# A head's softmax moved into the next head's block, a seventh pair in the seven-product phase, and 13 fillers a head in an attention trunk

## The chip, the cores and the metric

The kernel runs on one NeuronCore of a Trainium2 chip. The metric is the device time of one execution in microseconds (us); 2113.32 us is the median of three runs before the change. In this kernel a change under about 0.2% (4.2 us) can't be told from none.

## What is computed

Two layers work on a residual stream x of 1024 positions by 1024 features in float32. Layer 0 mixes by a short gated convolution, layer 1 by dilated attention with 16 heads of 64 dimensions; each is followed by a SwiGLU block of width 2816, and a norm ends the trunk. The change lies in the attention layer:

```python
qkv = (h @ w_qkv).reshape(bsz, seq, 3, N_HEADS, HEAD_DIM)
q, k, v = qkv[:, :, 0], qkv[:, :, 1], qkv[:, :, 2]
for window, dilation in BRANCHES:          # (128, 1), (512, 4), (2048, 16)
    o, l = dilated_branch(q, k, v, rel_bias, window, dilation)   # banded softmax(qk + bias) v, and its log-sum
    outs.append(o); lses.append(l)
alpha = jax.nn.softmax(jnp.stack(lses, axis=0), axis=0)
o = jnp.sum(alpha[..., None] * jnp.stack(outs, axis=0), axis=0)
return o.reshape(bsz, seq, D_MODEL).astype(h.dtype) @ w_out
```

## The kernel before

Activations lie transposed, features on the 128 partitions and positions along the free axis. Every float32 product that must be exact is made of three matmuls: each operand is split into a high and a low part (`split`, line 128: ScalarE copies the high part, VectorE subtracts it), and high by high, high by low and low by high are summed in a PSUM bank. Large products go by Strassen's seven-product scheme (class `Strassen`, products at lines 570 to 572) where two weight tiles can be paired; the rest go through `product` (lines 372 to 374). All instructions stand in the order in which the Python code issues them; each engine takes its own in that order. SBUF tiles come from a pool of 41 pages and some half pages, PSUM has 8 banks.

Q and K of the attention are made for pairs of heads (8 pairs). The class `QueryKey` makes the first `QK_PAIRS` pairs in a seven-product phase: 7 products of 4 k-tiles and 3 terms, 84 matmuls of 128x512 a pair, against 96 by `product`. Its results are scaled, split and written to DRAM by `emit` (lines 1139 to 1148), from where each head's block loads them.

After that come 17 blocks, one call of `slot(n, ...)` each, for n = 0 to 16. Block n holds three strands, interleaved by hand:

- `scores` of head n: score matmuls of q against k in eight steps (lines 1573 and 1574; first against `kca`, k regrouped by residue mod 4 for the two wide branches, then against `ka`), each followed by VectorE's additions of the bias out of the bank into `lf`, `lh`, `ld` and `lp` (lines 1584 to 1615), by maxima into `m`, and at the end by GpSimd's `partition_all_reduce` of m into mb (line 1627);
- `values` of head n-1: matmuls of the exponentials with the values (line 1646), whose sums and denominators ScalarE copies out as z and o (lines 1669 and 1670), which frees two banks;
- fillers, steps of the generator `dense`: the value projections v1 to v3 (20 steps a tile group, lines 1516 to 1518), Q and K of pairs 6 and 7 (`projections`, 36 steps a pair, of which 32 hold three matmuls), and the first half of the output product (`out_product`, 64 steps), whose banks VectorE adds to x at line 491.

`softmax(n)` is five pairs of operations: VectorE subtracts mb from `lf`, `lh`, `ld` and the two parts of `lp` (line 1635), and ScalarE takes the exponential (line 1636). Blocks 0 to 13 (`n <= LAG`) are of the lagged form: a first half of eight score steps with a filler each, and a second half in which the values of head n-1 run among the remaining fillers; there `softmax(n)` is issued at one go in the second half's step 3. From block 14 on scores and values share the first half, and `softmax(n)` stands in the second half's step 4.

`finish` scales a finished pair, `attended` writes it to DRAM, and `load_attended` with `halves` reads the first four pairs back and splits them (tiles `oin` to `w_lo`) ahead of the output product.

Of the kernel before, what the change touches and what calls it, by code (L numbers as in the profile page):

```python
# [20 lines left out]
H = 16  # L21
# [20 lines left out]
FFN_PAIRS, FFN_CHUNK = 9, 3  # L42
CONV_PAIRS, CONV_CHUNK, CO = 0, 1, 4
CONV, QK = "conv", "qk"
QK_PAIRS = 6
PAGES = 41
SOFT = 4
FIN0 = 2
AO_WIDE = 5
AO = 4  # L50
LAG = 13
FILL = (("v", 0), ("v", 1), ("v", 2), ("qk", 6), ("v", 3), ("qk", 7))
DEEP_ORDER = (1, 2, 5, 6, 7, 3, 4)


# [44 lines left out]
def trunk(ctx: ExitStack, tc: tile.TileContext, x, gains_in, cwi, ck, cwo, wqkv, wo, relb,  # L100
# [276 lines left out]
    def run(*gens):  # L377
        for _ in zip(*gens):
            pass
        for g in gens:  # L380
            for _ in g:
                pass
# [1096 lines left out]
    def attention(norm, qk):  # L1479
# [150 lines left out]
        def softmax(st):  # L1630
            lf, lh, ld, lp, mb = (st[n] for n in ("lf", "lh", "ld", "lp", "mb"))
            for dst, m in ((lf, mb), (lh, mb[:, HALF:]), (ld, mb),
                           (view(lp, 8, [[32, 16], [1, 24]]), view(mb, 8, [[32, 16], [1, 24]])),
                           (lp[:, HALF:], mb[:, HALF:])):
                nc.vector.tensor_tensor(out=dst, in0=dst, in1=m, op=ALU.subtract)
                nc.scalar.activation(dst, dst, AF.Exp)
                yield
# [72 lines left out]
                nc.vector.tensor_tensor(out=o, in0=o, in1=z, op=ALU.mult)  # L1710
                nc.gpsimd.dma_start(odram[p], o)

        put_off, ending = [], []
        OZ, acts = {}, {}

        def slot(n, dense, ndense, late=0, hook=iter(())):

            def other(k):
                for _ in range(k):
                    next(dense, None)  # L1720
# [25 lines left out]
            used = 0  # L1746
            if lagged:
                for i in range(8):
                    next(sc, None)
                    if n or i % 2:  # L1750
                        other(1)
                        used += 1
                    if a and ending and i == 0:
                        run(ending.pop())
                run(sc)
            else:
                if a == 0 and not late:
                    other(1)
                    used += 1
                for i in range(8):  # L1760
                    next(sc, None)
                    next(pv, None)
                    next(pv, None)
                    if i >= late and i % 2 == 0:
                        other(1)
                        used += 1
                run(sc)
                run(pv)
                if a == 0:
                    extra = finish(p - 1)  # L1770
                if a == 0 and n < H:
                    load_values(p)
            left = max(ndense - used, 0)
            for i in range(8):
                next(pv, None)
                next(pv, None)
                if i == (2 if n > LAG + 1 else 5):
                    attended()
                if not lagged and (i < FIN0 or i > SOFT):
                    next(extra, None)  # L1780
                if i in (1, 2):
                    next(later, None)
                if i < 4:
                    next(hook, None)
                if i == (3 if lagged else SOFT):
                    if n < H:
                        live[n] = new
                        run(softmax(new))
                other(left * (i + 1) // 8 - left * i // 8)
            run(pv)  # L1790
            run(extra)
# [48 lines left out]

        dense = fill()
        for n in range(H):
            if n == LAG - 1:
                done.update(load_attended(range(AO)))
            hook = halves() if n == LAG - 1 else iter(())
            slot(n, dense, 15, 3 if n == H - 2 else 0, hook)
            run(hook)
        acts.update(split_attended(load_attended(range(AO, 7))))
        ensure(ahead_ao)
        slot(H, dense, 15)  # L1850
        run(dense)
        return acts

# [203 lines left out]
```

## Time and profile before

| what | us |
|---|---|
| median of 3 runs (2112.34 to 2113.49) | 2113.32 |
| the profiled execution | 2113.6 |
| its span | 2111.8 |
| phase that makes Q and K, about 980 to 1095 | 115 |
| first score matmul of head 0 | at 1104.3 |
| first score matmul of head 15 | at 1385.0 |
| DMA share in the head blocks (1104 to 1406) | 0.77 |

The profile names engines PE (TensorE), PEld (its weight loads), DVE (VectorE), ACT (ScalarE), POOL (GpSimd) and SP (SyncE). A row of a single instruction gives its start and length in us, the engine, the line, the operation, the tile written and the tiles read, shape, and in brackets the idle time before it with what ended it. Matmuls are pipelined: a 128x512 matmul shows 0.39 us, but the next one starts 0.23 us later, so work is counted by the distance of starts.

### The profile page before, as it was taken

The page shows a single profiled execution, that of the slowest core. Times are in us where ns is not written, and L with a number is a line of the kernel's source. Part 1 is how long each engine was busy: PE and PEld are TensorE (multiplying, and loading weights), DVE is VectorE, ACT ScalarE, POOL GpSimd, SP SyncE. Part 2 cuts the span into 40 slices and gives each one's busy share as a digit, 9 for nine tenths or more (in the row PEclk, how much of TensorE's full clock was granted, in tenths as well). Part 3 has the DMA queues.
Part 4 walks back from the last instruction along what each step waited for, and adds up shares of the span by engine and source line. Part 5 has one row for each costly group of instructions (what it writes and reads, how often), then busy time and mean ns, then how long its engine had stood idle before and what let it go on. Part 6 is the DMA issues. An engine that isn't in the chain of part 4 may idle for free. (4 is left out here: it accounts for less than half of the span.)

```text
span 2111.8 us, 30764 instructions
## 1 busy us (share of the span) xinstructions
PE 2088.2 (99%) x11006; PEld 1796.4 (85%) x11006; DVE 1737.2 (82%) x3255; ACT 1021.1 (48%) x1868; POOL 236.8 (11%) x337
## 2 busy tenths in 40 slices
PE   9999999999999999999999999999999999999998
PEld 7788888888888888887799999988788888888887
DVE  8898769988888888968967687987998888888876
ACT  7433427443434554446545555555544434456435
POOL 1000000110101000010322222211011011001000
PEclk9999999999999999999999999999999999999999
DMA  7322643323333476351767777955223333358432
GB/s 221 95 95 70 229 135 75 105 100 110 115 100 107 155 206 203 121 157 65 244 210 190 170 184 191 250 190 140 70 90 105 105 106 105 115 187 244 158 95 80
DMA packets 141527, 300.77 MB, mean 142 GB/s; under 512 B 48252, under 2 KB 54478, under 8 KB 141376
## 3 DMA queue, kind: packets, MB, share of 16 engines
q1 hardware_dynamic: 107488, 201.94, 32.7%
q0 software_dynamic: 26256, 82.18, 12.3%
q10 hardware_dynamic: 7632, 14.70, 1.8%
q8 instruction: 87, 1.43, 0.3%
q14 instruction: 64, 0.52, 0.1%
HBM read 208.49 MB, written 82.93 MB: 138 GB/s over the span
## 5 line engine op out<-in xcount | busy, mean ns | idle before, releaser
L572 PE MATMUL bank<-b,w 128*128 128x512 f32 x1952 | 761.3, 390 | 5.1 <-DVE w L145 4.9
L570 PE MATMUL bank<-b,w 128*128 128x512 f32 x1952 | 761.7, 390 | 3.6 <-ACT w L144 2.3
L571 PE MATMUL bank<-b,w 128*128 128x512 f32 x1952 | 761.2, 390 | 0.6 <-DVE b L881 0.6
L572 PEld LDWEIGHTS bank<-b,w 128*128 128x128 f32 x1952 | 366.9, 188 | 85.6 <-DVE w L145 9.4
L570 PEld LDWEIGHTS bank<-b,w 128*128 128x128 f32 x1952 | 367.0, 188 | 80.1 <-ACT w L144 3.1
L571 PEld LDWEIGHTS bank<-b,w 128*128 128x128 f32 x1952 | 367.1, 188 | 75.6 <-DVE b L881 1.5
L144 ACT ACTIVATE w<-combo 128x512 fp32r<-128x512 f32 (+2 forms) x488 | 249.2, 540 | 237.8 <-DVE combo L192 220.6
L145 DVE TENSOR_TENSOR w<-combo,w 128x512 fp32r<-128x512 f32 (+2 forms) x488 | 276.5, 580 | 37.9 <-ACT w L144 37.1
L576 ACT ACTIVATE part<-bank 128x512 f32<-128x512 f32 x186 | 110.7, 595 | 377.7 <-PE bank L572 377.4
L145 DVE TENSOR_TENSOR w<-raw,w 128x512 fp32r<-128x512 f32 (+2 forms) x342 | 189.8, 576 | 36.3 <-ACT w L144 36.3
L580 DVE TENSOR_TENSOR part<-part,bank 128x256 f32<-128x256 f32 (+1 forms) x366 | 170.7, 496 | 29.5 <-PE bank L572 16.7
L144 ACT ACTIVATE w<-raw 128x512 fp32r<-128x512 f32 (+2 forms) x342 | 166.8, 530 | 45.4 <-PE bank L572 11.5
L372 PE MATMUL bank<-w_hi,w 128*128 128x512 f32 (+1 forms) x400 | 150.8, 377 | 0.1
L374 PE MATMUL bank<-w_hi,w 128*128 128x512 f32 (+1 forms) x400 | 149.3, 373 | 0.7 <-DVE w L145 0.7
L373 PE MATMUL bank<-w_lo,w 128*128 128x512 f32 (+1 forms) x400 | 149.0, 372 | 0.0
L491 DVE TENSOR_TENSOR x<-x,bank 128x512 f32<-128x512 f32 (+1 forms) x104 | 66.2, 642 | 61.2 <-PE bank L374 60.8
L800 DVE TENSOR_TENSOR x<-x,bank 128x512 f32<-128x512 f32 x136 | 92.6, 681 | 28.8 <-PE bank L572 28.8
L192 DVE TENSOR_TENSOR combo<-raw 128x512 f32<-128x512 f32 (+1 forms) x172 | 111.1, 647 | 0.0
L374 PEld LDWEIGHTS bank<-w_hi,w 128*128 128x128 f32 x400 | 75.3, 188 | 14.8 <-DVE w L145 1.6
L563 DVE TENSOR_TENSOR b<-hin,b 128x512 fp32r<-128x512 f32 x126 | 79.4, 684 | 9.4 <-ACT b L562 9.4
L372 PEld LDWEIGHTS bank<-w_hi,w 128*128 128x128 f32 x400 | 75.5, 189 | 12.6 <-ACT w L144 0.5
L373 PEld LDWEIGHTS bank<-w_lo,w 128*128 128x128 f32 x400 | 75.5, 189 | 12.1
(241 smaller groups left out, 3452.8 us busy)
## 6 DMA issues: line engine op xcount, KB each, us to landing
hin<-part SPq DMA_DIRECT2D x126, 256.0 KB
raw<-in_ffn_w_gate SPq DMA_DIRECT2D x44, 512.0 KB
raw<-in_ffn_w_up SPq DMA_DIRECT2D x44, 512.0 KB
part<-sum POOLq DMA_DIRECT2D x72, 256.0 KB, 2.3
raw<-in_ffn_w_down SPq DMA_DIRECT2D x48, 384.0 KB
raw<-in_attn_w_qkv SPq DMA_DIRECT2D x27, 512.0 KB
raw<-in_conv_w_in SPq DMA_DIRECT2D x24, 512.0 KB
part<-part POOLq DMA_DIRECT2D x36, 256.0 KB, 2.6
```

Of the source, the lines that this page charges most:

```text
L144: nc.scalar.activation(hi, src, AF.Copy)
L145: eng.tensor_tensor(out=lo, in0=src, in1=hi, op=ALU.subtract)
L192: eng.tensor_tensor(out=c, in0=a, in1=b, op=op)
L372: nc.tensor.matmul(b, whi[:, a], ahi[:, s], start=first, stop=False)
L373: nc.tensor.matmul(b, whi[:, a], alo[:, s], start=False, stop=False)
L374: nc.tensor.matmul(b, wlo[:, a], ahi[:, s], start=False, stop=last)
L570: nc.tensor.matmul(b, hi[:, a], bhi, start=start and k == 0, stop=False, skip_group_check=True)
L571: nc.tensor.matmul(b, hi[:, a], blo, start=False, stop=False, skip_group_check=True)
L572: nc.tensor.matmul(b, lo[:, a], bhi, start=False, stop=k == n - 1, skip_group_check=True)
L576: nc.scalar.activation(t, b, AF.Copy)
L580: nc.vector.tensor_tensor(out=t, in0=t, in1=b, op=ALU.add)
L800: nc.vector.tensor_tensor(out=X[n][:, half(h)], in0=X[n][:, half(h)], in1=b, op=ALU.add)
```

## The change

Three constants change. `QK_PAIRS` goes from 6 to 7, and pair 6 leaves the list of fillers. The fillers per block go from 15 to 13 (`DENSE`), and in a lagged block ten of these stand in the first half: one at each score step and a second one at steps 3 and 7 (`EXTRA`). In the lagged blocks `softmax(n)` is no longer run in block n; its generator is kept in `due` and stepped once ahead of each score step of block n+1. Block 13 still runs it at once, since block 14 has another form. `finish` of the pair before is issued at score step 4 instead of 0. The attended tiles are loaded and split in block 11 instead of 12.

```diff
-QK_PAIRS = 6
+QK_PAIRS = 7
...
-FILL = (("v", 0), ("v", 1), ("v", 2), ("qk", 6), ("v", 3), ("qk", 7))
+EXTRA = (3, 7)
+FILL = (("v", 0), ("v", 1), ("v", 2), ("v", 3), ("qk", 7))
+DENSE = 13
...
-        put_off, ending = [], []
+        put_off, ending, due = [], [], [iter(())]
...
             if lagged:
                 for i in range(8):
+                    next(due[0], None)
                     next(sc, None)
-                    if n or i % 2:
-                        other(1)
-                        used += 1
-                    if a and ending and i == 0:
+                    k = 1 + (i in EXTRA) if n else i % 2
+                    other(k)
+                    used += k
+                    if a and ending and i == 4:
                         run(ending.pop())
...
-                if i == (3 if lagged else SOFT):
-                    if n < H:
-                        live[n] = new
-                        run(softmax(new))
+                if i == (3 if lagged else SOFT) and n < H:
+                    live[n] = new
+                    due[0] = softmax(new)
+                    if n >= LAG:
+                        run(due[0])
...
-            if n == LAG - 1:
+            if n == LAG - 2:
                 done.update(load_attended(range(AO)))
-            hook = halves() if n == LAG - 1 else iter(())
-            slot(n, dense, 15, 3 if n == H - 2 else 0, hook)
+            hook = halves() if n == LAG - 2 else iter(())
+            slot(n, dense, DENSE, 3 if n == H - 2 else 0, hook)
...
-        slot(H, dense, 15)
+        slot(H, dense, DENSE)
```

What this does to the order on the engines, at the three places that the prediction speaks of. Lines of the new kernel are two higher than those of the old one there.

ScalarE, around the end of block 3, before:

```order
L1636 ACTIVATE lf<-lf 128x1024
L1636 ACTIVATE lh<-lh 128x512
L1636 ACTIVATE ld<-ld 128x1024
L1636 ACTIVATE lp<-lp 128x16x24
L1636 ACTIVATE lp<-lp 128x512
L1669 ACTIVATE z<-bank 64x512
L1670 ACTIVATE o<-bank 64x512
L1669 ACTIVATE z<-bank 64x512
L1670 ACTIVATE o<-bank 64x512
```

and in the change:

```order
L1671 ACTIVATE z<-bank 64x512
L1672 ACTIVATE o<-bank 64x512
L1671 ACTIVATE z<-bank 64x512
L1672 ACTIVATE o<-bank 64x512
L1638 ACTIVATE lf<-lf 128x1024
L1523 ACTIVATE v<-bank,scales 128x256
L1638 ACTIVATE lh<-lh 128x512
L1638 ACTIVATE ld<-ld 128x1024
L1638 ACTIVATE lp<-lp 128x16x24
L1638 ACTIVATE lp<-lp 128x512
```

The copies of z and o out of the value banks stood behind the five exponentials of the next head and now stand ahead of them; evictions of the value projection (v) fall among the exponentials.

VectorE, head 0's softmax and the first adds of head 1, before:

```order
L1635 TENSOR_TENSOR lf<-lf,mb 128x1024
L1635 TENSOR_TENSOR lh<-lh,mb 128x512
L1635 TENSOR_TENSOR ld<-ld,mb 128x1024
L1635 TENSOR_TENSOR lp<-lp,mb 128x16x24
L1635 TENSOR_TENSOR lp<-lp,mb 128x512
```

and in the change:

```order
L1637 TENSOR_TENSOR lf<-lf,mb 128x1024
L1586 TENSOR_TENSOR lf<-bank,bias 128x4x64 x2
L1637 TENSOR_TENSOR lh<-lh,mb 128x512
L1586 TENSOR_TENSOR lf<-bank,bias 128x4x64 x2
L1637 TENSOR_TENSOR ld<-ld,mb 128x1024
L1595 TENSOR_TENSOR lh<-bank,bias 128x512
L1600 TENSOR_TENSOR m<-lf,lh 128x512
L1637 TENSOR_TENSOR lp<-lp,mb 128x16x24
L1612 TENSOR_TENSOR ld<-bank,bias 128x16x16
L1617 TENSOR_TENSOR lp<-bank,bias 128x16x16
L1637 TENSOR_TENSOR lp<-lp,mb 128x512
```

The five subtractions stood together; now the bias adds of the next head stand between them. The first subtraction, which waits for the all-reduce, stays ahead of the next head's first add.

VectorE, where the four attended tiles are split, before (ahead of head 12's softmax):

```order
L1624 TENSOR_TENSOR m<-m,lp 128x512
L145 TENSOR_TENSOR w_lo<-oin,w_hi 128x1024 x4
L1635 TENSOR_TENSOR lf<-lf,mb 128x1024
L1635 TENSOR_TENSOR lh<-lh,mb 128x512
L1635 TENSOR_TENSOR ld<-ld,mb 128x1024
```

and in the change (ahead of head 11's):

```order
L1626 TENSOR_TENSOR m<-m,lp 128x512
L147 TENSOR_TENSOR w_lo<-oin,w_hi 128x1024 x4
L1712 TENSOR_TENSOR o<-o,z 128x1024
L1143 SCALAR_TENSOR_TENSOR kq<-bank,rstd 128x512
L1637 TENSOR_TENSOR lf<-lf,mb 128x1024
L1586 TENSOR_TENSOR lf<-bank,bias 128x4x64 x2
L1149 TENSOR_TENSOR kq_lo<-kq,kq_hi 128x512
L1637 TENSOR_TENSOR lh<-lh,mb 128x512
```

A pair's scaling (o by z) and a Q part of pair 7 moved from behind the softmax to ahead of it. On GpSimd's queue the eight DRAM writes of pair 6 move from the head blocks to the phase that makes Q and K; on SyncE's queue its two weight loads move there too, and the loads of four attended tiles come one block earlier.

## The prediction

> **What bounds the kernel now.** I read the busy line first, then the table of stretches, then the waits of TensorE and VectorE in the attention stage, and last single rows in order of time, because a busy share says nothing about which wait ends last.
>
> ```profile
> span 2111.8 us, 30764 instructions
> PE 2088.2 (99%) x11006; PEld 1796.4 (85%) x11006; DVE 1737.2 (82%) x3255; ACT 1021.1 (48%) x1868; POOL 236.8 (11%) x337
> ...
> 980.00:1095.00 115.00, 114.12 (x554) 95.53 (x553) 102.67 (x158) 61.46 (x105) 30.40 (x55) 1.00 0.55 182
> ...
> 1153.50:1175.50 22.00, 20.43 (x161) 20.02 (x160) 16.88 (x29) 14.55 (x22) 5.65 (x7) 0.92 0.72 177
> 1175.50:1251.10 75.60, 75.60 (x562) 71.32 (x561) 58.52 (x104) 40.68 (x57) 21.20 (x20) 1.00 0.81 194
> ...
> PE bank L1573 <- ACT o L1670: 1.6, 2, 1.1
> ```
>
> The stretch rows give length, then busy time of PE, PEld, DVE, ACT and POOL, then the granted clock. TensorE is busy without a gap in the phase that makes Q and K (980 to 1095) and in the head blocks (from 1104), except in one block: 1153.5 to 1175.5 lasts 22.0 us, holds 1.57 us of idle TensorE and a clock of 0.92. Its neighbours carry the same kind of work at clock 1.00. So in both stages a matmul less is time less, as long as the other engines keep up.
>
> ```profile
> 1251.12 0.29 PE L1573 MATMUL bank<-qa,kca 128*128 128x256 f32 x1
> 1269.44 0.29 PE L1573 MATMUL bank<-qa,kca 128*128 128x256 f32 x1
> ...
> 1212.77 0.28 PE L1573 MATMUL bank<-qa,kca 128*128 128x256 f32 x1
> 1232.26 0.28 PE L1573 MATMUL bank<-qa,kca 128*128 128x256 f32 x1
> ...
> 1344.17 0.28 PE L1573 MATMUL bank<-qa,kca 128*128 128x256 f32 x1
> 1364.71 0.28 PE L1573 MATMUL bank<-qa,kca 128*128 128x256 f32 x1
> ```
>
> These are the first score matmuls of neighbouring blocks, so each pair is a block's length: 18.3 us with value fillers (block 8), 19.5 us with Q/K fillers (block 6), 20.5 us with out-product fillers (block 13).
>
> VectorE's loop is next. A head's chain is: subtract the maximum, add the biases to the next head's scores, take maxima, wait for GpSimd's all-reduce, subtract again.
>
> ```profile
> 1117.00 1.23 DVE L1635 TENSOR_TENSOR lf<-lf,mb 128x1024 f32<-128x1024 f32 x1 [3.54 <-POOL mb L1627]
> ...
> 1128.05 0.69 DVE L1624 TENSOR_TENSOR m<-m,lp 128x512 f32<-128x512 f32 x1
> 1132.16 1.23 DVE L1635 TENSOR_TENSOR lf<-lf,mb 128x1024 f32<-128x1024 f32 x1 [3.42 <-POOL mb L1627]
> ...
> DVE lf L1635 <- POOL mb L1627: 38.2, 13, 3.5
> DVE w_lo L145 <- ACT w_hi L144: 8.0, 4, 2.3
> DVE kq_lo L1147 <- ACT kq_hi L1144: 5.6, 5, 1.9
> ```
>
> Without other work one turn is 11.74 us of VectorE (1117.00 to 1128.74) and 3.42 us of waiting, 15.2 us. That is 3.1 us under the shortest block, and every split or scaling that VectorE does beside it eats into this margin.
>
> **The change part by part.** *Pair 6 leaves the fillers.* Its 32 steps with matmuls are three 128x512 matmuls each.
>
> ```profile
> 1227.62 0.48 PE L372 MATMUL bank<-b,w_hi 128*128 128x512 f32 x1
> 1227.93 0.39 PE L373 MATMUL bank<-b,w_hi 128*128 128x512 f32 x1
> 1228.16 0.40 PE L374 MATMUL bank<-b,w_lo 128*128 128x512 f32 x1
> 1228.40 0.38 PE L1646 MATMUL bank<-ld,vx 128*128 128x128 f32 x2
> 1228.62 0.39 PE L1646 MATMUL bank<-lp,vx 128*128 128x128 f32 x2
> ...
> 1229.20 0.48 PE L372 MATMUL bank<-b,w_hi 128*128 128x512 f32 x1
> ```
>
> Two steps start 1.58 us apart, and between them lie four double value matmuls 0.22 us apart, 0.88 us. A step costs 0.70 us, and 32 steps are 22.4 us off TensorE's line. The four steps that only evict carry no matmul.
>
> *Pair 6 enters the seven-product phase* with 84 matmuls (7 products, 4 k-tiles, 3 terms).
>
> ```profile
> 1075.81 0.39 PE L570 MATMUL bank<-b,w 128*128 128x512 f32 x1
> ...
> 1076.49 0.39 PE L570 MATMUL bank<-b,w 128*128 128x512 f32 x1
> ```
>
> Three matmuls start in 0.68 us, so 84 take 19.05 us. VectorE has some 15 us of new work in them (4 sums, 7 splits, 3 partial sums, 4 scalings, 4 low parts, at about 0.69 us, the low part's row further down) and was busy 103 of 115 us in that phase with TensorE at 114, so I put the phase's extra wait at 0; bounds are 0 and 0.9 us, the idle time that the phase has now. The weight DMAs only come earlier. Both moves together: 3.35 us less.
>
> *The softmax steps move between the next block's scores.* The number of instructions is the same. What moves on ScalarE is the place of the eviction of the value sums (z and o), which free two banks.
>
> ```profile
> 1158.60 0.28 PE L1518 MATMUL bank<-w_hi,b 128*128 128x256 f32 x1
> ...
> 1159.94 0.38 PE L1573 MATMUL bank<-qa,ka 128*128 128x256 f32 x1 [1.07 <-ACT o L1670]
> ...
> 1161.17 0.48 PE L1573 MATMUL bank<-qa,ka 128*128 128x256 f32 x1 [0.51 <-ACT o L1670]
> 1161.45 0.42 PE L1574 MATMUL bank<-ql,ka 128*128 128x256 f32 x1
> ...
> 1159.92 0.59 ACT L1669 ACTIVATE z<-bank 64x512 f32<-64x512 f32 x1
> ```
>
> Twice in block 3 TensorE waits for the copies L1670, which stand behind five exponentials that wait for VectorE; then its matmuls take 0.42 instead of 0.28 us for some 3.4 us (the 0.92 above). With the evictions ahead of the exponentials (the order shown in the section on the change) these copies, four of 0.59 us, are done some 2.4 us into the block, before any exponential, and this block should shrink to its neighbours: 22.0 - 18.4 = 3.6 us. Bounds: 0, if the banks run out elsewhere, and 3.6.
>
> That half-speed stretch came after 1.6 us of idle. The Trainium skill, "TensorE: Matmul & The Clock Gate", section on the clock gate, has the array drop to half clock only after an idle window of about 3.4 us. This trace disagrees (0.92 in the row above after two waits of 1.07 and 0.51 us); by the page a wait of some 2 us would cost itself alone.
>
> *Thirteen fillers instead of fifteen a block.* The steps are only spread thinner (220 in place of 256), so TensorE's sum is already counted; what shrinks is the cover over VectorE's loop. A block with value fillers loses two steps of 0.72 us (six matmuls 0.12 us apart), four in five of them with matmuls: 18.3 - 1.15 = 17.2 us. With Q/K it is 19.5 - 1.4 = 18.1, with the out product 20.5 - 1.4 = 19.1 us. The plain loop of 15.2 fits under all of them. The rest that VectorE has to do there:
>
> ```profile
> L1710 DVE TENSOR_TENSOR o<-o,z 128x1024 f32<-128x1024 f32 x7 | 8.5, 1218 | 0.0
> L145 DVE TENSOR_TENSOR w_lo<-raw,w_hi 128x1024 fp32r<-128x1024 f32 x8 | 10.8, 1359 | 8.0 <-ACT w_hi L144 8.0
> L1147 DVE TENSOR_TENSOR kq_lo<-kq,kq_hi 128x512 fp32r<-128x512 f32 x8 | 5.5, 690 | 5.6 <-ACT kq_hi L1144 5.6
> ...
> 1335.83 0.69 DVE L1624 TENSOR_TENSOR m<-m,lp 128x512 f32<-128x512 f32 x1
> 1336.43 6.32 DVE L145 TENSOR_TENSOR w_lo<-oin,w_hi 128x1024 fp32r<-128x1024 f32 x4
> 1342.68 1.21 DVE L1635 TENSOR_TENSOR lf<-lf,mb 128x1024 f32<-128x1024 f32 x1
> ```
>
> In the new order the scalings (1.22 us) fall into the 3.4 us wait and are free. Blocks 5 and 8 have two weight splits among the adds, 15.2 + 2.7 = 17.9 us, 0.7 over the block, made up in the next one. The hard place is block 11 to 14: the four splits of attended tiles (6.3 us) now come there together with a scaling and a Q/K part (1.22 + 0.68) ahead of the next subtraction. Block 11's adds start about 0.7 us after its first score matmul; 10.5 us of the loop and 1.4 us of Q/K parts end at 12.6, the splits and the two others at 20.8, which is 2.7 us into block 12 (18.1 long). From there 11.74 + 1.37 + 3.42 = 16.5 us lead to 0.1 us into block 13, and 11.74 + 1.94 (two adds to x and a split) + 3.42 = 17.1 to 1.9 us before block 14.
>
> ```profile
> 1361.81 1.23 DVE L1635 TENSOR_TENSOR lf<-lf,mb 128x1024 f32<-128x1024 f32 x1 [2.83 <-POOL mb L1627]
> ...
> 1363.07 1.06 ACT L1636 ACTIVATE lf<-lf 128x1024 f32<-128x1024 f32 x1 [8.79 <-DVE lf L1635]
> ...
> 1365.19 1.06 PE L1646 MATMUL bank<-lf,vx 128*128 128x128 f32 x8
> ```
>
> Block 14 opens with values that need the exponential; it ends 2.3 us after the subtraction starts, and TensorE wants it 0.5 us into the block. Today it is 1.1 us early. Then it is there 0.1 us before it is wanted, with no cover left. If each low part on the way also waits for ScalarE as in the waits above (13.6 us over 9 waits, 1.5 each), the lag grows by two or three of these and the wait is up to 3.6 us. Between 0 and 3.6 I take 1.2 us, nearer the lower end, since those waits hit 9 of 16 low parts.
>
> **Sum**, against the profiled execution's own 2113.6 us (span 2111.8), which is 0.3 over the median of 2113.3: -22.4 + 19.05 - 3.6 + 1.2 = -5.75, so 2107.9 for such an execution and **2107.6 us** against the median.
>
> **The rivals.** *Nothing waits at all:* block 14 costs 0; 2113.3 - 6.95 = 2106.4. The plain loop's 15.2 us speaks for it, the four splits against it.
>
> *The late blocks eat the gain:* 3.6 us at block 14 and, as in block 3, a half-clock stretch of 3.4 us behind it, 1.7 us more: -22.4 + 19.05 - 3.6 + 3.6 + 1.7 = -1.65, 2111.7 us, which is no change that can be told. The lower cover speaks for it; against it, blocks 12 and 13 give back 2.6 and 2.0 us of lag. By the page's rule on the clock this case would be 2110.0.
>
> *VectorE's loop becomes the bound of the blocks* (the slower side). One mechanism: the exponentials' subtractions and the bias adds now alternate, so a late score, a late ScalarE half or a late all-reduce stops both. Beside the plain loop a head has some 40 us / 15 = 2.7 us of other VectorE work (the groups above and the out product's adds) and, by the waits, 13.6 / 15 = 0.9 us of waiting for ScalarE. If none of it falls into the all-reduce's wait, the turn is 15.2 + 2.7 + 0.9 = 18.8 us against 17.8 us of matmuls a block on average. It decides from 2.6 us of unhidden work a head; at 18.8 the price is 13 blocks x 1.0 = 13 us, 2113.3 - 6.95 + 13 = 2119.4 us. Against it: in the new order the scalings and half of the splits stand in that wait.
>
> *The saving isn't there:* the seventh pair stalls its own phase, which holds four x tiles' operands longer in a full page pool; 0.9 us idle as now for each of two more products would take the time to 2109.4. Against it: VectorE has 12 us to spare in that phase now, and its weights still come two products ahead.
>
> **How the numbers follow.** My forecast 0.50, nothing waits 0.15, the late blocks 0.20, VectorE's loop 0.10, the phase 0.05. What a measurement can tell from no change is 0.2%, 4.2 us, so faster is under 2109.1. The forecast's own range is 2106.0 to 2109.8; 0.43 of its 0.50 lie under 2109.1, with the first rival 0.58 faster; VectorE's loop alone is slower, 0.10; the rest 0.32. The range has to hold 8 of 10: down to the removal of every wait with a little more (2104.5), up past the late blocks (2113.5); it leaves out VectorE's loop and little else.
>
> **What would show it.** Right: 96 matmuls fewer on the out-of-phase Q/K lines and 84 more on the lines of the seven-product phase, a Q/K phase 19 us longer at unchanged clock, value-filler blocks of 17.2 us, no wait for the copies of o in block 3, the subtraction of lf within 2 us of a block's first score. Wrong: waits of TensorE for lf's or lp's exponential or for VectorE's adds in blocks 5 to 9; blocks of 18 us and more with value fillers; a clock under 1.00 anywhere from block 11 on. My forecast falls if the blocks don't get shorter by the two steps, or if the Q/K phase grows by more than 20 us.

## The result and the profile after

| | before | changed |
|---|---|---|
| median of 9 runs each, us | 2113.11 (2111.79 to 2114.36) | 2108.13 (2107.62 to 2109.48) |
| profiled execution, us | 2113.6 | 2108.13 |
| its span, us | 2111.8 | 2106.4 |

The ratio of the times is 0.9978, with a 95% interval of 0.997 to 0.9986: faster by 5.0 us, just over the 0.2% that can be told from no change. The forecast was 2107.6.

The busy line of the changed kernel:

```profile
span 2106.4 us, 30797 instructions
PE 2084.8 (99%) x10994; PEld 1794.3 (85%) x10994; DVE 1743.6 (83%) x3267; ACT 1027.8 (49%) x1876; POOL 239.9 (11%) x337
```

In the table of groups (busy us, mean ns of one, idle time ahead), one line of each of the two Q/K paths and the all-reduce's, first of the kernel before:

```profile
L570 PE MATMUL bank<-b,w 128*128 128x512 f32 x1952 | 761.7, 390 | 3.6 <-ACT w L144 2.3 <-ACT b L880 0.9 <-ACT part L576 0.4
L372 PE MATMUL bank<-b,w_hi 128*128 128x512 f32 x64 | 28.0, 437 | 0.0
L1627 POOL PARTITION_ALL_REDUCE mb<-m x16 | 52.4, 3272 | 108.4 <-DVE m L1624 72.9 <-PE bank L1646 22.7 <-PE bank L1518 7.1
```

and of the changed one:

```profile
L572 PE MATMUL bank<-b,w 128*128 128x512 f32 x1980 | 772.7, 390 | 1.9 <-ACT w L146 1.1 <-ACT part L578 0.4 <-ACT b L882 0.3
L374 PE MATMUL bank<-b,w_hi 128*128 128x512 f32 x32 | 13.4, 420 | 0.0
L1629 POOL PARTITION_ALL_REDUCE mb<-m x16 | 55.9, 3494 | 144.6 <-DVE m L1626 83.9 <-PE bank L1648 22.9 <-PE bank L1520 14.1
```

The pair moved as the diff says. Each of the three lines of the seven-product phase has 28 matmuls more (84 in all) and each of the three filler lines 32 fewer (96), and TensorE's count is lower by 12. The all-reduce's mean is longer, 3.49 us for 3.27: nothing in the prediction had that.

Where the time went, in the table of stretches. Before: the first 26 to 34 us, from a matmul of the convolution to head 0's first score, and from there to the first matmul after the heads' work that both traces show alike:

```profile
26.00:34.00 8.00, 7.33 (x26) 5.61 (x25) 7.73 (x13) 8.00 (x13) 1.78 (x2) 0.79 0.26 50
288.38:1104.28 815.90, 812.39 (x4014) 687.80 (x4013) 686.16 (x1278) 393.01 (x757) 89.48 (x155) 1.00 0.44 138
...
1104.28:1493.47 389.19, 387.61 (x2653) 357.72 (x2652) 303.32 (x527) 213.41 (x317) 86.68 (x75) 1.00 0.70 181
```

and the same stretches of the changed kernel, with blocks 3 and 14 behind them:

```profile
26.00:34.00 8.00, 7.33 (x32) 5.93 (x32) 7.60 (x13) 8.00 (x12) 1.78 (x2) 1.00 0.26 50
286.81:1121.84 835.03, 831.57 (x4099) 703.69 (x4097) 700.82 (x1300) 401.18 (x771) 93.78 (x163) 1.00 0.44 140
...
1121.84:1487.32 365.48, 363.15 (x2558) 338.22 (x2556) 295.19 (x517) 212.39 (x311) 85.45 (x67) 1.00 0.72 182
...
1168.00:1184.90 16.90, 16.90 (x148) 16.90 (x147) 12.75 (x24) 10.38 (x16) 7.12 (x6) 1.00 0.92 199
...
1361.40:1382.90 21.50, 19.17 (x126) 17.26 (x125) 18.17 (x32) 13.54 (x20) 3.77 (x2) 1.00 0.61 158
```

The way to head 0 is 835.03 - 815.90 = 19.1 us longer, the heads' stretch 365.48 - 389.19 = 23.7 us shorter, together -4.6 us. A further 1.6 us between the two profiled executions (288.38 against 286.81) lies before anything that was changed, where the one of before had a clock of 0.79 and this one 1.00; it is no part of the effect, for the second profile of the kernel before (the last experiment) has 1.00 there. Behind the heads' work the changed execution takes 0.7 us longer to its end; the run with the splits one block earlier doesn't, so that is put down to the single execution, and the medians differ by 5.0 us.

Block 3 (1168.0) is 16.9 us, was 22.0, with no idle TensorE and the clock at 1.00. Block 14 (1361.4) is 21.5 us and holds 2.3 us of idle TensorE. The waits of TensorE in the attention stage (total, times, longest) are these two, and none of them is for the copies of o:

```profile
PE bank L1648 <- ACT lf L1638: 1.4, 1, 1.4
PE bank L1575 <- DVE x L493: 0.9, 1, 0.9
```

Their rows:

```profile
1363.44 1.16 PE L1648 MATMUL bank<-lf,vx 128*128 128x128 f32 x8 [1.41 <-ACT lf L1638]
...
1366.90 0.33 PE L1575 MATMUL bank<-qa,kca 128*128 128x128 f32 x1 [0.92 <-DVE x L493]
```

VectorE in order of time shows how block 14 comes to them (start, duration; the bracket is the idle time ahead and what ended it). Block 12 begins at 1323.7, 13 at 1342.6, 14 at 1361.4:

```profile
1318.77 6.32 DVE L147 TENSOR_TENSOR w_lo<-oin,w_hi 128x1024 fp32r<-128x1024 f32 x4
1325.02 1.21 DVE L1712 TENSOR_TENSOR o<-o,z 128x1024 f32<-128x1024 f32 x1
1326.15 0.68 DVE L1143 SCALAR_TENSOR_TENSOR kq<-bank,rstd 128x512 f32<-128x512 f32 x1
1326.75 1.21 DVE L1637 TENSOR_TENSOR lf<-lf,mb 128x1024 f32<-128x1024 f32 x1
...
1329.61 0.69 DVE L1149 TENSOR_TENSOR kq_lo<-kq,kq_hi 128x512 fp32r<-128x512 f32 x1 [0.98 <-ACT kq_hi L1146]
...
1341.25 2.08 DVE L147 TENSOR_TENSOR w<-raw,w 128x512 fp32r<-128x512 f32 x1
...
1344.15 1.23 DVE L1637 TENSOR_TENSOR lf<-lf,mb 128x1024 f32<-128x1024 f32 x1 [0.23 <-POOL mb L1629]
...
1361.08 1.23 DVE L1637 TENSOR_TENSOR lf<-lf,mb 128x1024 f32<-128x1024 f32 x1 [3.41 <-POOL mb L1629]
...
1365.03 1.22 DVE L1712 TENSOR_TENSOR o<-o,z 128x1024 f32<-128x1024 f32 x1
1366.16 0.68 DVE L493 TENSOR_TENSOR x<-x,bank 128x512 f32<-128x512 f32 x1
```

Head 11's subtraction starts 3.05 us into block 12, head 12's 1.5 us into block 13, and head 13's (1361.08) only 0.3 us before block 14, whose values want its exponential at once. Then the scaling of o and, behind it, the addition to x stand in VectorE's order; that addition frees the bank for which a score matmul waits 0.92 us.

### The profile page after: what moved, and what is told of

Its sections match the earlier page's. It is cut to its first block, busy times and chain, and to the rows that moved or that the text cites. A ratio compares the mean times of both kernels' runs of the same rounds, so it can differ in the third digit from the quotient of the medians.

```text
span 2106.4 us, 30797 instructions
## 1 busy us (share of the span) xinstructions
PE 2084.8 (99%) x10994; PEld 1794.3 (85%) x10994; DVE 1743.6 (83%) x3267; ACT 1027.8 (49%) x1876; POOL 239.9 (11%) x337
## 4 chain that ended last, share of the span: by engine, by line
PE 47%; DVE 4%; ACT 1%; issue 1%; DMA 1%; POOL 0%; DVEq 0%; ACTq 0%; POOLq 0%
PE bank L574 9%; PE bank L572 9%; PE bank L573 9%; PE bank L1648 4%; PE bank L374 2%; PE bank L376 2%; PE bank L375 2%; PE bank L1518 1%; PE bank L1520 1%; PE bank L1519 1%; PE bank L664 1%; PE bank L667 1%; PE bank L666 1%; PE bank L1576 1%; PE bank L1575 1%
## 5 line engine op out<-in xcount | busy, mean ns | idle before, releaser
L574 PE MATMUL bank<-b,w 128*128 128x512 f32 x1980 | 772.7, 390 | 4.7 <-DVE w L147 4.4
L572 PE MATMUL bank<-b,w 128*128 128x512 f32 x1980 | 772.7, 390 | 1.9 <-ACT w L146 1.1
L573 PE MATMUL bank<-b,w 128*128 128x512 f32 x1980 | 772.2, 390 | 0.0
L574 PEld LDWEIGHTS bank<-b,w 128*128 128x128 f32 x1980 | 372.1, 188 | 87.1 <-DVE w L147 9.7
L572 PEld LDWEIGHTS bank<-b,w 128*128 128x128 f32 x1980 | 372.5, 188 | 79.1 <-ACT w L146 2.0
L573 PEld LDWEIGHTS bank<-b,w 128*128 128x128 f32 x1980 | 372.5, 188 | 75.9 <-DVE b L883 0.5
L582 DVE TENSOR_TENSOR part<-part,bank 128x256 f32<-128x256 f32 (+1 forms) x369 | 172.6, 497 | 32.1 <-PE bank L574 17.4
```

Of the source, the lines that this page charges most:

```text
L572: nc.tensor.matmul(b, hi[:, a], bhi, start=start and k == 0, stop=False, skip_group_check=True)
L573: nc.tensor.matmul(b, hi[:, a], blo, start=False, stop=False, skip_group_check=True)
L574: nc.tensor.matmul(b, lo[:, a], bhi, start=False, stop=k == n - 1, skip_group_check=True)
L582: nc.vector.tensor_tensor(out=t, in0=t, in1=b, op=ALU.add)
```

## The experiments

Times are medians. The kernel before was run beside each group: 2112.55 us (the runs up to the four fillers in block 14), 2112.45 (uneven fillers to eight pairs and both edits), 2112.32 (one split a block, and the kernel before once more), 2112.56 (two splits in block 9, and the scalings on GpSimd). A ratio is to the kernel before of the same group, with its 95% interval in brackets. The changed kernel was measured against 2113.11, so two runs of different groups are compared by what each gained. Of the diffs, "..." marks left-out lines.

**The softmax move alone**: the kernel before with the steps `due` of the change, but six pairs, fifteen fillers, one filler a score step, `finish` at step 0 and the splits in block 12, as before.

```diff
-        put_off, ending = [], []
+        put_off, ending, due = [], [], [iter(())]
...
+                    next(due[0], None)
                     next(sc, None)
...
-                if i == (3 if lagged else SOFT):
-                    if n < H:
-                        live[n] = new
-                        run(softmax(new))
+                if i == (3 if lagged else SOFT) and n < H:
+                    live[n] = new
+                    due[0] = softmax(new)
+                    if n >= LAG:
+                        run(due[0])
```

> The kernel before with the softmax steps moved into the next block alone: six pairs, fifteen fillers, splits in block 12 as before. My theory (block 3's wait for the copies of o is removed by the order on ScalarE, worth 3.6 us, nothing else moves): 2113.1 - 3.6 = 2109.5 us, block 3 as long as its neighbours at clock 1.00, no wait of over 0.3 us in the head blocks. Rival 1 (all of the gain is the pair's): 2113.1. Rival 2 (the alternation makes VectorE's loop late with fifteen fillers too): a wait for lf's exponential at block 14 like the changed kernel's 1.4 us, 2111 or more.

Measured 2111.25 us, ratio 0.9991 (0.9983 to 1.0): 1.3 us faster, with an interval that reaches no change. The theory's 2109.5 is missed, and the time is that of the second rival. The two largest waits of TensorE in the attention stage of this kernel:

```profile
PE bank L1573 <- DVE x L491: 0.9, 1, 0.9
PE bank L1646 <- ACT lf L1636: 0.4, 1, 0.4
```

The waits for the copies of o are gone and block 3 is 18.35 us, 3.6 less than in the kernel before. Block 14 has new waits of 1.3 us with fifteen fillers too: it is 21.84 us for 20.28. The term of 3.6 us is there, and 1.6 of it is given back at block 14 by the move itself.

**The pair and the thirteen fillers alone**: the changed kernel with each head's softmax in its own block, as before; `finish` at step 4 and the splits in block 11 stay.

```diff
-                    due[0] = softmax(new)
-                    if n >= LAG:
-                        run(due[0])
+                    run(softmax(new))
```

> The changed kernel with softmax run at one go in its own block as before; seven pairs, thirteen fillers, splits in block 11 stay. My theory (the move of the softmax is what lets the blocks be shorter, because the copies of z and o stand behind five exponentials otherwise): waits for the copies of o of 1 to 2 us in two to eight blocks, 2112 to 2122 us. Rival 1 (the move of the softmax is worth only block 3's 3.6 us): 2108.1 + 3.6 = 2111.7 with one such wait. Rival 2 (the pair does it all): 2108 to 2110.

Measured 2120.37 us, ratio 1.0038 (1.0024 to 1.0051), in the theory's range. The largest entry of TensorE's waits in the attention stage:

```profile
PE bank L1575 <- ACT o L1672: 7.1, 5, 3.4
```

and in the table of stretches the one that holds block 3 (1169.6 to 1192.5):

```profile
1167.00:1192.00 25.00, 21.08 (x167) 20.67 (x166) 17.19 (x32) 12.68 (x18) 8.60 (x6) 0.93 0.87 181
```

Alone the pair saves nothing and loses 7.8 us: shorter blocks make the copies of o late in five places, one by 3.4 us, and block 3's clock is 0.93. So the two halves aren't a sum: -1.3 and +7.8 alone, -5.0 together. The softmax move is worth some 12 us to a kernel that has thirteen fillers.

**The attended tiles split one block earlier** (block 10 in place of 11).

```diff
-            if n == LAG - 2:
+            if n == LAG - 3:
-            hook = halves() if n == LAG - 2 else iter(())
+            hook = halves() if n == LAG - 3 else iter(())
```

> The changed kernel with the four attended tiles loaded and split in block 10 instead of 11. My theory (the 6.3 us of splits make VectorE late, and the lag reaches block 14 after two blocks): one more block to make the lag up, subtraction of head 13 some 1.5 us earlier against block 14's start, the waits of 1.41 and 0.92 us there shrink to under 0.8 together, 2106.3 us. Rival (thirteen fillers leave too little cover between block 13's maxima and block 14's values, whatever was late before): the two waits stay, 2108.1.

Measured 2108.29 us, ratio 0.9979 (0.997 to 0.9988): a miss for my theory. Head 13's subtraction came 0.7 us before block 14 for 0.3, and the waits were 1.0 and 0.9 us. The lag only begins a block earlier: head 10's subtraction comes 2.7 us into block 11 (1309.4 against 1306.7) and head 11's still 2.6 us into block 12, for 3.05.

**Four fillers ahead of block 14's scores.**

```diff
-                if a == 0 and not late:
-                    other(1)
-                    used += 1
+                if a == 0:
+                    other(4 if late else 1)
+                    used += 4 if late else 1
```

> The changed kernel with four fillers ahead of block 14's scores and values instead of none; they come out of the rest of that block. My theory (block 14 waits for an exponential 1.41 us and then for a bank 0.92 us, and 2.8 us of matmuls ahead cover both): 2108.1 - 2.3 = 2105.8 us. Rival (the wait is only moved: the second half of block 14 loses four fillers and block 15 waits instead): 2107.5 to 2108.5 with a wait of 1 to 2 us at block 15.

Measured 2107.86 us, ratio 0.9978 (0.997 to 0.9987). The waits in order of time on TensorE:

```profile
1366.78 1.16 PE L1648 MATMUL bank<-lf,vx 128*128 128x128 f32 x8 [0.74 <-DVE x L493]
...
1382.51 0.71 PE L1648 MATMUL bank<-lf,vx 128*128 128x128 f32 x4 [0.94 <-ACT lf L1638]
```

The wait for the exponential went from block 14 to block 15, which starts at 1380.9, and the one for the addition stayed: the rival. Fillers moved forward only take cover from the next block; what is late is VectorE, not the order on TensorE.

**Twelve fillers up to block 7, fourteen from block 8.**

```diff
-            slot(n, dense, DENSE, 3 if n == H - 2 else 0, hook)
+            slot(n, dense, 12 if n < 8 else 14, 3 if n == H - 2 else 0, hook)
...
-        slot(H, dense, DENSE)
+        slot(H, dense, 14)
```

> The changed kernel with uneven fillers: 12 a block in blocks 0 to 7, 14 from block 8 on, the same total. Theory (block 14's two waits, 2.65 us in excess, are lag that VectorE gathered in blocks 11 to 13, and longer blocks give it back): blocks 8 to 13 are some 0.7 us longer each, head 13's subtraction starts 3 us or more before block 14 (0.3 in the changed kernel), both waits are gone, and blocks 1 to 7 get 0.7 us shorter without a wait: 2105.3 to 2106.8. Rival 1 (VectorE's loop becomes the bound): blocks 1 to 7 of 16.2 us don't cover a loop of 15.2 with two weight splits or a scaling, TensorE waits there, 2107.5 to 2110. Rival 2 (the end of block 13 has too little cover whatever came before): the waits at block 14 stay and the time is that of the changed kernel, 2108.

Measured 2109.16 us, ratio 0.9985 (0.9976 to 0.9994): a time of the first rival without its mechanism, since the short blocks of 16.2 us did not wait. The late blocks did become longer, but a Q part of pair 7 now fell ahead of the splits, and they wait for ScalarE in turn:

```profile
1320.81 1.23 DVE L147 TENSOR_TENSOR w_lo<-oin,w_hi 128x1024 fp32r<-128x1024 f32 x1 [1.65 <-ACT w_hi L146]
1322.81 1.23 DVE L147 TENSOR_TENSOR w_lo<-oin,w_hi 128x1024 fp32r<-128x1024 f32 x1 [0.78 <-ACT w_hi L146]
```

Head 11's subtraction is 5.6 us into block 12 there (1328.2 against 1322.6), and TensorE waits 0.8 us in block 12 and 1.5 us in block 14. An unequal share of fillers also moves the fillers' own work on VectorE against the splits, which no theory had counted.

**The scalings left out.** The pairs 0 to 6 are not multiplied by their reciprocal sums, so their attention is not normalised; the transfer of o stays.

```diff
                 p, o, z = put_off.pop()
-                nc.vector.tensor_tensor(out=o, in0=o, in1=z, op=ALU.mult)
                 nc.gpsimd.dma_start(odram[p], o)
```

> The changed kernel without the multiplication of o by the reciprocal sums for pairs 0 to 6 (so the attention's output isn't normalised for them; the transfer of o stays). The prediction's step (the scalings fall into the all-reduce's wait and are free): time as the changed kernel, 2107.6 to 2108.5, and head 13's subtraction still 0.3 us or so before block 14. Theory now (they lengthen the all-reduce beside them from 3.22 to 4.04 us, and the one in block 11 stands behind the splits, ahead of the subtraction): all all-reduces in the blocks last 3.2 us apart from those beside splits, the lag in block 12 is 1.2 to 2 us smaller, block 14's waits fall from 2.65 to about 1 us: 2106.3 to 2107.3.

Measured 2106.14 us, ratio 0.9969 (0.9957 to 0.9981), just under the theory's range. The all-reduce's group:

```profile
L1629 POOL PARTITION_ALL_REDUCE mb<-m x16 | 52.7, 3292 | 158.6 <-DVE m L1626 81.5 <-issue 20.9 <-PE bank L1648 18.0
```

TensorE's one wait in the blocks:

```profile
PE bank L1648 <- ACT lf L1638: 0.3, 1, 0.3
```

and block 14's stretch:

```profile
1361.60:1381.10 19.50, 19.17 (x127) 17.33 (x125) 15.91 (x30) 13.39 (x20) 3.65 (x2) 1.00 0.60 160
```

Seven instructions of 1.2 us cost the changed kernel 1.3 to 2.0 us: the gain over the kernel before is 6.3 us here and 5.0 there, and from head 0's first score to the end of the heads' work the two traces differ by 2.0 us. Blocks 1 to 10 are as long without them as with them (16.8 to 18.1), so there they are free as predicted, with the all-reduce back at 3.2 us. All of the traces' 2.0 us is at block 14: head 11's subtraction is 1.9 us into block 12 for 3.05, head 13's 1.4 us before block 14, and the addition to x has no scaling ahead of it.

**The eighth pair too**, with eleven fillers and the attended tiles' splits in block 10.

```diff
-QK_PAIRS = 7
+QK_PAIRS = 8
-FILL = (("v", 0), ("v", 1), ("v", 2), ("v", 3), ("qk", 7))
-DENSE = 13
+FILL = (("v", 0), ("v", 1), ("v", 2), ("v", 3))
+DENSE = 11
...
-            if n == LAG - 2:
+            if n == LAG - 3:
...
-            hook = halves() if n == LAG - 2 else iter(())
+            hook = halves() if n == LAG - 3 else iter(())
```

> The changed kernel with pair 7 too in the products ahead of the heads, 11 fillers a block and the attended tiles' splits one block earlier. By matmuls alone it saves another 22.4 - 19.05 = 3.35 us: 2104.7 if nothing waits. Theory (the rival of the prediction with VectorE's loop as the bound holds from here on): blocks with value fillers would be 16.9 - 1.15 = 15.8 us, the loop of 15.2 with splits and scalings averages 17 or more, so TensorE waits for exponentials or adds in several blocks: 2108.5 to 2116. Rival (cover is enough, VectorE's extra work falls into its waits): 2104.5 to 2106.5 with waits only near block 14.

Measured 2118.06 us, ratio 1.0026 (1.0016 to 1.0035). That is above both ranges, and the theory's place is wrong too, for the blocks with value fillers don't wait. Stretches of this kernel, blocks 0 to 9, then block 10, then block 11:

```profile
1143.40:1298.00 154.60, 154.59 (x1336) 154.48 (x1335) 121.37 (x234) 92.26 (x130) 45.70 (x36) 1.00 0.82 191
1298.00:1318.00 20.00, 17.38 (x144) 16.79 (x142) 15.80 (x27) 13.12 (x18) 6.83 (x3) 0.98 0.69 184
1318.00:1339.00 21.00, 20.09 (x121) 17.96 (x121) 18.18 (x30) 12.06 (x17) 7.43 (x6) 0.85 1.04 243
```

Nine blocks of 15.4 to 16.4 us behind a first of 10.2 pass with TensorE busy for 154.59 of 154.60 us, over a VectorE loop of 15.2. The loss begins where the out product's first matmuls wait 2.3 and 0.9 us for the attended tiles' low parts, since the fillers now reach it before those are split; then the clock is at 0.85. The waits for exponentials that the theory had come later: 1.8 us in block 14 and 2.3 us in block 15, both for `lf`.

**Both edits, uneven fillers and early splits.**

```diff
-            slot(n, dense, DENSE, 3 if n == H - 2 else 0, hook)
+            slot(n, dense, 12 if n < 8 else 14, 3 if n == H - 2 else 0, hook)
...
-            if n == LAG - 2:
+            if n == LAG - 3:
...
```

> The changed kernel with both edits: fillers 12 and 14 as in the uneven run, and the attended tiles' splits one block earlier (block 10). Theory (lag): no wait at block 14, head 13's subtraction 4 us or more ahead, 2105.3 to 2106.6, no better than the uneven fillers alone. Rival (the splits earlier only move VectorE's late stretch to shorter blocks): a wait in blocks 10 to 12, 2107 to 2109.

Measured 2108.99 us, ratio 0.9982 (0.9973 to 0.999). Block 14 has no wait here, as the theory said. Three others came in block 11 and at the start of block 12, for VectorE's adds (1.1 and 0.8 us) and for kca (0.9), behind block 10's splits, one of which waits 2.96 us for its high part: the rival.

**The splits spread, one a block** in blocks 8 to 11, each tile loaded at the start of its block.

```diff
-            for q, t in done.items():
-                first[q] = split(t)
+            for q in list(done):
+                first[q] = split(done.pop(q))
                 yield
...
-            if n == LAG - 2:
-                done.update(load_attended(range(AO)))
-            hook = halves() if n == LAG - 2 else iter(())
+            if LAG - 5 <= n < LAG - 1:
+                done.update(load_attended([n - LAG + 5]))
+            hook = halves()
```

> The changed kernel with the four early attended tiles loaded and split one a block, in blocks 8, 9, 10 and 11, in place of four in block 11. Theory (block 14's waits are lag of VectorE that begins in block 11, where 6.3 us of splits and a scaling stand between head 11's maximum and its subtraction, longer than the all-reduce's 3.2 to 4.0 us that they could hide in): one split of 1.4 us, with a scaling 2.6, fits in the all-reduce's time, head 11's subtraction comes about 1 us into block 12 or earlier, head 13's 1.5 us or more before block 14, and the waits of 2.65 us fall below 0.7: 2105.4 to 2106.5. Rival (as when all four came one block earlier: whatever is done, the full all-reduce at the end of block 13 behind short blocks leaves the exponential late): subtraction of head 13 within 0.8 us of block 14, waits of 2 us, 2107.5 to 2108.5.

Measured 2112.21 us, ratio 0.9995 (0.9986 to 1.0004): above both ranges. Waits of SyncE's queue at the loads of attended tiles and of TensorE in the blocks:

```profile
SPq L1800 <- PE bank L1520: 9.9, 1, 9.9
...
SPq L1800 <- PE bank L376: 6.8, 1, 6.8
...
PE bank L1648 <- ACT lf L1638: 2.7, 1, 2.7
PE bank L1575 <- ACT kca L1559: 1.3, 1, 1.3
```

and VectorE in block 12, in order of time:

```profile
1342.30 0.69 DVE L493 TENSOR_TENSOR x<-x,bank 128x512 f32<-128x512 f32 x1 [3.25 <-DMA x<-spill]
```

Head 11's subtraction did come 0.9 us into block 12 (1330.6 against 1329.7), as the theory has it. The lead was lost in the same block: a load that stands early in SyncE's order waits there for a free page and holds up what is behind it, so head 9's kca and then the tile x arrive late, and VectorE stands 3.25 us at an addition with all subtractions behind it.

**Two splits in block 9, two in block 11, loaded behind the block's other loads.**

```diff
-            for q, t in done.items():
-                first[q] = split(t)
-                yield
+            for q in qs:
+                done.update(load_attended([q]))
+            yield
+            yield
+            for q in qs:
+                yield
+                first[q] = split(done[q])
...
-            if n == LAG - 2:
-                done.update(load_attended(range(AO)))
-            hook = halves() if n == LAG - 2 else iter(())
+            hook = halves({LAG - 4: (0, 1), LAG - 2: (2, 3)}.get(n, ()))
```

> The changed kernel with two attended tiles split in block 9 and two in block 11, each pair loaded in the second half of its own block, behind that block's loads of Q, K and biases in SyncE's queue. Theory (block 11's pile of splits and scaling starts the lag; the run with one split a block lost its gain because its loads stood in SyncE's queue ahead of others and waited there for pages up to 9.9 us, so that kca and x came late): head 11's subtraction about 1 us into block 12, no wait of VectorE for x, head 13's subtraction 1 us or more before block 14, block 14's waits below 1 us: 2105.6 to 2106.8. Rival (spread loads hold pages and delay x or the next head's K in any order): a wait of TensorE for kca in blocks 9 to 12 or of VectorE for x in block 12, 2109 to 2113.

Measured 2112.26 us, ratio 0.9999 (0.999 to 1.0008), in the rival's range. Now the split in block 9 waits, and head 9's subtraction behind it. ScalarE's high part of that tile, and VectorE's low part, which needs it:

```profile
1288.09 1.06 ACT L146 ACTIVATE w_hi<-oin 128x1024 fp32r<-128x1024 f32 x1 [4.78 <-DMA oin<-odram]
...
1289.18 1.23 DVE L147 TENSOR_TENSOR w_lo<-oin,w_hi 128x1024 fp32r<-128x1024 f32 x1 [5.19 <-PE bank L1576]
```

The bracket of the low part names TensorE, but the high part ends at 1289.15, just before it starts. The load left SyncE's queue at 1281.22, after a wait of at most 0.7 us there, and the high part got its tile 6.9 us later, in a stretch in which the DMA engines were fully busy (share 1.00 from 1281 to 1289). So here it was not a page but the time from the load's issue to its landing. Of these two orders, the early loads held up SyncE's queue and the late ones didn't arrive in time. That the lag can be taken away by spreading the splits is not shown.

**The scalings on GpSimd.**

```diff
-                nc.vector.tensor_tensor(out=o, in0=o, in1=z, op=ALU.mult)
+                nc.gpsimd.tensor_tensor(out=o, in0=o, in1=z, op=ALU.mult)
```

> The changed kernel with the scalings of o done on GpSimd in place of VectorE. Theory (the scaling in block 11 stands ahead of head 11's subtraction and those in the blocks lengthen the all-reduce; leaving them out altogether gave 2106.1): every all-reduce lasts 3.2 us apart from those beside splits, head 13's subtraction is about 1 us before block 14, block 14's waits about 0.5 us: 2106 to 2107. Rival (GpSimd's multiplication of 128x1024 is long, and VectorE's instructions beside it lengthen as its low parts do beside an all-reduce): subtractions and adds beside it take half as long again, the lag is the same or larger, 2107.5 to 2111.

Measured 2130.14 us, ratio 1.0084 (1.007 to 1.0097): far above both ranges. GpSimd in blocks 4 and 7 in order of time, then VectorE in the same blocks:

```profile
1193.75 2.77 POOL L1712 TENSOR_TENSOR o<-o,z 128x1024 f32<-128x1024 f32 x1 [6.93 <-ACT lp L1638]
...
1245.92 3.24 POOL L1629 PARTITION_ALL_REDUCE mb<-m  x1 [6.40 <-DMA vx<-vdram]
...
1194.85 2.21 DVE L1621 TENSOR_TENSOR m<-lf,ld 128x512 f32<-128x512 f32 x1
...
1249.19 1.23 DVE L1637 TENSOR_TENSOR lf<-lf,mb 128x1024 f32<-128x1024 f32 x1 [10.13 <-POOL mb L1629]
```

The multiplication takes 2.4 to 2.8 us for 1.2, and a maximum beside it 2.21 us for 0.68. Far worse, in block 7 head 6's all-reduce starts 7 us after that head's last maximum, behind a transfer, and VectorE waits 10.1 us. Block 7 lasts 24.7 us for 17.6, and block 12 grows as much, 25.8 us for 18.9. How the scaling's place makes that transfer late, and what happens in block 12, was not followed further.

**The kernel before once more**, one profile.

> The kernel before, unchanged, for a second profile of it. If block 3's loss belongs to the kernel, the wait of the first score matmuls for the copies of o is there again, 1.6 us in two waits, and block 3 lasts 20.2 to 22 us, with or without a stretch at half clock. If it was an accident of one execution, block 3 is about 18.4 us and the term of 3.6 us in the prediction falls.

Measured 2112.66 us. Block 3 of this second execution:

```profile
1152.60:1174.60 22.00, 20.44 (x161) 20.02 (x160) 16.88 (x29) 14.67 (x22) 5.77 (x7) 0.92 0.70 177
```

and its wait:

```profile
PE bank L1573 <- ACT o L1670: 1.6, 2, 1.1
```

The same length, clock and wait as in the first profile: the 3.6 us belong to the kernel.

## Why the prediction was right, point by point

- *Pair 6 in the seven-product phase, +19.05 us*: 19.1 measured. The phase's extra wait is nil: idle TensorE on the way to head 0 is 835.03 - 831.57 = 3.46 us, before 815.90 - 812.39 = 3.51. The rival with a stalling phase falls.
- *Fillers, -22.4, and block 3, -3.6*: the heads' stretch is 23.7 us shorter, and with the excess of the two waits at block 14 (2.65 us more than the usual distance between starts) added back it is 26.35; the two terms make 26.0. Blocks with value fillers are 16.8 to 17.7 us for a predicted 17.2; the first profile's 3.6 us came again in a second one, and the softmax move alone recovers them.
- *Block 14, +1.2*: 2.65 us, within its bounds of 0 to 3.6, and the one mis-sized term. Head 13's subtraction came 0.3 us before block 14 for a predicted 1.9. Of these 1.6 us, VectorE's chain is only 0.3: from block 11's start (1306.4) it took 54.7 us for 54.4. Its parts are off in both directions: head 11's subtraction 20.4 us into the chain for 20.8, the turn to head 12's 17.4 us for 16.5 (0.98 of it a wait of kq_lo for ScalarE's kq_hi, which I had named and put at nought or 1.5), the turn to head 13's 16.9 for 17.1. The other 1.3 us is TensorE: blocks 11, 12 and 13 are 17.3, 18.9 and 18.8 us long, together 55.0 us for the 56.3 that I had put there, most of it in block 11, which I had at 18.1. That makes the first wait, 1.4 us. The second, 0.9 us, was no step of mine: the addition to x that frees a bank stands in VectorE's order behind five subtractions and a scaling, and those come late together.
- *The subtraction of lf within 2 us of a block's first score*, one of my signs of being right, doesn't hold: it comes 2.7 to 2.9 us into blocks 2, 3 and 6, and 3.05 into block 12. TensorE waits in none of these four blocks; the lag of block 12 is the one that reaches block 14.
- *The scalings are free*: true of blocks 1 to 10, false for block 11, where I had counted 1.22 us, and for block 14, where I had counted none. Left out, they give 1.3 to 2.0 us.
- *Nothing waits at all* (2106.4): false. The nearest case is the run without the scalings, with one wait of 0.3 us left and less work: 2106.14.
- *The late blocks eat the gain* (2111.7): right in its place and in part of its size, 2.65 of 3.6 us, but without the half-clock stretch: block 14's clock is 1.00. By the rule of the Trainium skill's page "TensorE: Matmul & The Clock Gate", section on the clock gate (half clock only after an idle window of about 3.4 us), none was due; but by the same rule block 3 of the kernel before would have none either, and it had it in both profiles.
- *VectorE's loop as the bound* (2119.4): false for the blocks with fillers of values. With eight pairs they shrank to 15.4 and 16.2 us without a wait. In the changed kernel VectorE binds only at block 14, behind the work that is piled up between a maximum and the next subtraction in block 11.

What stays open is whether block 14's 2.65 us can be had without leaving work out. Six orders were tried; the best, four fillers ahead of block 14, is 2107.86 us, which can't be told from the changed kernel.

## What to carry over

When two engines go in lock step, moving one engine's work (here a softmax) may gain little by itself and yet be what lets another change pay: the pair alone cost 7.8 us, the move alone gave 1.3, both gave 5.0. Count the slack of an in-order engine between the two points that another engine sees (last maximum to next subtraction), not as a mean a block: a wait of 3.4 us for the all-reduce hides a scaling of 1.2 us, but not where four splits of 6.3 us have filled it already. Work out the length of the covering blocks one by one as well: VectorE's chain was forecast within 0.3 us, and three blocks that came out 1.3 us shorter in all made most of the error at block 14. Before you move a load earlier, look at what its queue waits for: a load without a free page stops those behind it.

## What the hardware showed that was not expected

- VectorE's work on two tiles and GpSimd's all-reduce hinder each other, and the one that starts later is the longer. In GpSimd's order, the all-reduces of the heads in blocks 2, 3 and 12 of the changed kernel:

```profile
1167.59 3.22 POOL L1629 PARTITION_ALL_REDUCE mb<-m  x1 [18.00 <-PE bank L1648]
...
1182.75 4.04 POOL L1629 PARTITION_ALL_REDUCE mb<-m  x1 [6.63 <-DVE m L1626]
...
1340.89 3.22 POOL L1629 PARTITION_ALL_REDUCE mb<-m  x1 [9.75 <-DMA vx<-vdram]
```

  In block 3 a scaling starts 0.26 us ahead of it (1182.49) and lasts its usual 1.22 us; the all-reduce takes 4.04 us for 3.22, and in the run without the scalings it takes 3.2 there. The w split of 1341.25 above starts 0.36 us behind an all-reduce (1340.89), which lasts 3.22; the split takes 2.08 us where one without company takes 0.68. Two additions to x beside the same all-reduce, whose second input is a bank, keep their usual 0.68. The Trainium skill, "SBUF — State Buffer", section on who interferes with whom, says that a VectorE instruction with two SBUF inputs contends with a GpSimd instruction that reads SBUF, and that the order of issue decides which of them blocks. The runs agree in both, though a VectorE instruction isn't held for the all-reduce's whole length: 1.4 us of 3.22.
- The drop of the clock doesn't follow the length of the wait. Waits of 1.07 and 0.51 us gave 0.92 in block 3 of the kernel before, twice; 1.41 and 0.92 us gave 1.00 in block 14 of the changed one. Single waits of nearly one length differ too: 1.87 us gave 0.93 in block 6 of the pair alone (1220 to 1245), 1.82 us gave 1.00 in block 14 of the kernel with eight pairs (1373 to 1393). What decides is open. In block 3 the two waits end 1.2 us apart (1159.94 and 1161.17), in block 14 3.5 us apart (1363.44 and 1366.90), but no run was made to test that this matters.
